# A two-layer hybrid transformer on one core: the first stage's loads, row products and prefills in another order

## The chip, the cores and the metric

The kernel runs on one core of a Trainium2 chip. The metric is the device time of one execution in microseconds (us). Names: PE is TensorE (the matmuls), DVE is VectorE, ACT is ScalarE, SP the engine whose queue issues the loads. On each engine instructions stand in an order that is fixed when the kernel is built.

## The reference, cut to what matters

Two layers work on 512 tokens (256 context, 256 latent) of width 2048. Only the start of the first layer concerns us: from a condition vector come a scale, a shift and a gate per channel, the tokens are normalised, scaled and shifted to `h`, and `h` is multiplied by a wide weight matrix.

```python
def adaln(cond, w, b):
    m = jax.nn.silu(cond) @ w + b
    return jnp.split(m, 3, axis=-1)
...
        shift, scale, gate = adaln(c, w_ada[l], b_ada[l])
        shift_c, scale_c, gate_c = adaln(c_ctx, w_ada[l], b_ada[l])
        h_lat = rms_norm(x, norm_gain[l]) * (1.0 + scale[:, None]) + shift[:, None]
        h_ctx = rms_norm(ctx, norm_gain[l]) * (1.0 + scale_c) + shift_c
...
    a_q, a_ff, a_fb, a_i, b_q, b_k, b_v, b_zf, b_zb, gate = jnp.split(h @ w_in, cuts, axis=-1)
```

All is float32. To keep that precision, an operand of a matmul is split into a high word (a cast) and a low word (what the cast left), and each product is three matmuls: high by high, high by low, low by high.

## The kernel before, in words

The channels form 16 tiles of 128, `h` is held with channels on the partitions, and tile k of `h` can be used as soon as its own scale and shift exist. So the first stage (`with tc.tile_pool(name="startup")`) goes through the tiles in nine chunks (`CHUNKS`, L40): two of one tile, seven of two. For each chunk `ch` the loop of L408 does this:

- **rows** (L312, `mx` is its sum): 16 small float32 matmuls of the condition with the scale and shift columns of this chunk. Their weights are eight tiles `ap`, loaded into a ring of eight buffers (`ADA_BUFS`). From chunk 2 on four column tiles are wanted; three go this way, the fourth as **dots** (L295) on DVE: two loaded tiles `ad`, four products of 128x1024 (`aj`, `ad`).
- **v_mms** (L249): the products of the chunk before with the value weights (`wvh`, `wvl`): 12 matmuls a tile.
- **mods** (L323) and **make_h0** (L349): the row sums are copied to `rs` by ACT, turned by PE, summed by DVE, and give `gs` and `mod`; ACT makes `ht` and its high word `h`, DVE the low word.
- **wave_q** (L367): the chunk before times two more weight tiles (`wqh`, `wql`), 6 matmuls a tile.
- **wave_w** (L359): loads and splits the `wv` and `wq` weights of this chunk for the next turn. There is one buffer for each (`WAVE_BUFS`), so the cast of `wqh` waits until wave_q has read the old one.
- **fill**: work of a later stage, the gate projections, of which `FILL` (L46) lists the part and up to which tile of `h` it goes. It is `proj` (L206) with a weight load (`rawfill`), its cast (`whfill`, ACT) and its low word (`wlfill`, DVE), and three matmuls for each tile, in the order high by high, high by low, low by high.

Before the loop stand the loads of the 16 tiles `x`, the rows of chunk 0, the squares of `x` on ACT (L388), and their sum over the channels on PE (`ss`). All loads go through SP's one queue; the code's order and the builder's scheduler set the order in which they stand, as for every engine.

Of the kernel before, what the change touches and what calls it, by code (L numbers as in the profile page):

```python
# [8 lines left out]
F32 = mybir.dt.float32  # L9
# [8 lines left out]
P = 128  # L18
# [20 lines left out]

CHUNKS = ((0,), (1,), (2, 3), (4, 5), (6, 7), (8, 9), (10, 11), (12, 13), (14, 15))  # L40
WAVE_BUFS = 1
CUT = (0, 4, 0, 0, 0, 0, 0, 0, 0)
SQ_TAGS = ("wh", "wl", "raw", "wh", "wl", "raw", "wh", "wl")
ADA_BUFS = 8
DOT_BUFS = 3
FILL = ((), tuple((p, 2) for p in range(6)), (), ((0, 6), (1, 6)), ((2, 6),), ((3, 8),), ((4, 8),), ((5, 8),), ())  # L46
GLA_WAITS = (4, 2, 2, 3)
NORM_WAITS = {"k": 2, "q": 3}
ATT_WAITS = (6, 2, 3, 2, 2, 2)
# [16 lines left out]
def dit_two_layers(ctx: ExitStack, tc, xT, cc, crow, vecs, w_as, w_as3, w_ad, w_ab, w_wv, w_wq, w_e, w_zz, w_a2, w_eo, w_o, w_oo,  # L66
# [58 lines left out]
        nc.sync.dma_start(raw[:, :n], src)  # L125
        return raw[:, :n]

    def load_split(src, name, eng=None):
        raw = load(src, "raw" + name)
        n = raw.shape[-1]  # L130
        wh = wp.tile([P, 1024], F32R, tag="wh", name="wh" + name, bufs=WH_BUFS)[:, :n]
        wl = wp.tile([P, 1024], F32R, tag="wl", name="wl" + name, bufs=WL_BUFS)[:, :n]
        split(raw, wh, wl, eng)
        return wh, wl
# [63 lines left out]
    def make_h(layer, k, c, t, rstd):  # L198
        seg, shift = segs[c], mod[:, layer, k, c:c + 1]
        dve.scalar_tensor_tensor(t, xt[k][:, seg], gs[:, layer, k, c:c + 1], rstd[:, seg], ALU.mult, ALU.mult)  # L200
        act.activation(hh[k][:, seg], t, AF.Identity, bias=shift)
        dve.scalar_tensor_tensor(hl[k][:, seg], t, shift, hh[k][:, seg].bitcast(F32), ALU.add, ALU.subtract)

    partial = {}

    def proj(units, c0, width, name, h_hi=None, h_lo=None, part=None, k1=KT, eng=None, early=None):  # L206
        a, b = h_hi or hh, h_lo or hl
        sofar, k0 = partial.get(part, (None, 0))
        ps = (acc if k1 == KT else aux)(name)
        for half in range(2):  # L210
            ks, ke = max(k0, 8 * half), min(k1, 8 * half + 8)
            if ks >= ke:
                if k1 == KT:
                    tick(2)
                continue
            o = 8 * half
            wh, wl = load_split(units[half][:, (ks - o) * P:(ke - o) * P], f"{name}_{half}", eng)
            for k in range(ks, ke):
                w1, w2 = wh[:, (k - ks) * P:(k - ks + 1) * P], wl[:, (k - ks) * P:(k - ks + 1) * P]
                x1, x2 = a[k][:, c0:c0 + width], b[k][:, c0:c0 + width]  # L220
                pe.matmul(ps[:, :width], w1, x1, start=(k == k0), stop=False)  # L221
# [56 lines left out]
    with tc.tile_pool(name="startup", bufs=1) as sp:  # L278
# [7 lines left out]
        sb0 = sp.tile([P, 2, D], F32, name="sb0")  # L286
        for c in range(2):
            for j in range(4):
                ps = acc(f"sb0_{c}_{j}")
                for i in range(4):  # L290
                    pe.matmul(ps[:, i * P:(i + 1) * P], view(c32, (4 * j + i) * 32 + c, (0, P)), ident,
                              start=True, stop=True)
                dve.tensor_copy(sb0[:, c, j * T:(j + 1) * T], ps)

        def dots(ch):  # L295
# [16 lines left out]
        def rows(ch, mx, u0, u1):  # L312
            n = len(on_pe(ch)) * P
            for u in range(u0, u1):
                raw = sp.tile([P, 768], F32, tag="ap", name=f"ap{ch}_{u}", bufs=ADA_BUFS)[:, :2 * n]
                nc.sync.dma_start(raw, (w_as if ch < 2 else w_as3)[8 * (ch if ch < 2 else ch - 2) + u])
                for i in range(2):
                    k = u * 2 + i
                    g = 32 * (k % 4)
# [4 lines left out]
        def mods(ch, mx, pd):  # L324
            tiles = on_pe(ch)
            n = len(tiles)
            rs = sp.tile([P, T], F32, tag="rs", name=f"rs{ch}")
            act.copy(rs[:, :n * P], mx[:, :n * P])
            for i in range(n):
                pe.transpose(mx[:, i * P:(i + 1) * P], rs[:, i * P:(i + 1) * P], ident)  # L330
            m4 = sp.tile([P, 4, 2], F32, tag="m4", name=f"m4_{ch}")
            dve.tensor_reduce(m4[:, :n, :], view(mx, 0, (128, n), (1, 2), (32, 4)), AX.X, ALU.add)
            for i, (f, k) in enumerate(tiles):
# [15 lines left out]
        def make_h0(ch):  # L349
            for k in CHUNKS[ch]:  # L350
                new_h(0, k)
                t = sp.tile([P, T], F32, tag="scr", name=f"ht0_{k}", bufs=3)
                for c in range(2):
                    act.activation(t[:, segs[c]], xt[k][:, segs[c]], AF.Identity, bias=mod[:, 0, k, c:c + 1],
# [1 line left out]
                act.copy(hh[k], t)  # L356
                dve.tensor_sub(hl[k], t, hh[k].bitcast(F32))

        def wave_w(ch, what, src, n):  # L359
            k0, nk = CHUNKS[ch][0], len(CHUNKS[ch])  # L360
            src = src[k0 // 2][:, (k0 % 2) * n:(k0 % 2 + nk) * n]
            raw = load(src, f"{what}r{ch}")
            wh, wl = [sp.tile([P, 2 * n], F32R, tag=f"{what}{x}", name=f"{what}{x}{ch}", bufs=WAVE_BUFS)[:, :nk * n]
                      for x in "hl"]
            split(raw, wh, wl, dve)
            return wh, wl

        def wave_q(ch, w2h, w2l):
            for i in range(2):
                for kk, k in enumerate(CHUNKS[ch]):  # L370
# [3 lines left out]
                    pe.matmul(wq[i], w1, hl[k], start=False, stop=False)  # L374
                    pe.matmul(wq[i], w2, hh[k], start=False, stop=(k == KT - 1))

        ss0 = aux("ss0")
        for k in range(KT):
            t = rp.tile([P, T], F32, tag=f"r{(k + 8) % KT}", name=f"x0_{k}")
            nc.sync.dma_start(t, xT[k])  # L380
            xt[k] = t
            if k == 7:
                mx = aux("mx0")
                rows(0, mx, 0, 8)
        for k in range(KT):
            if k % 2 == 0:
                sq = wp.tile([P, 2, T], F32, tag=SQ_TAGS[k // 2], name=f"sq0_{k}", bufs=3)
            act.activation(sq[:, k % 2, :], xt[k], AF.Square)  # L388
            if k % 2 and k < KT - 1:
                dve.tensor_tensor(sq[:, 0, :], sq[:, 0, :], sq[:, 1, :], ALU.add)  # L390
                pe.matmul(ss0, ones, sq[:, 0, :], start=(k == 1), stop=False)
        for i in range(2):
            pe.matmul(ss0, ones, sq[:, i, :], start=False, stop=(i == 1))
        wn = wave_w(0, "wv", w_wv, T), wave_w(0, "wq", w_wq, 256)
# [744 lines left out]
```

## Time and profile before

| | us |
|---|---|
| median of 3 runs | 1758.53 (1756.43 to 1761.26) |
| the profiled execution | 1759.63 |
| its span, first to last instruction | 1757.7 |
| PE busy in the span | 1735.1 (99%) |
| DVE busy | 1283.0 (73%) |
| ACT busy | 760.5 (43%) |

The span is what the profile sees of the execution. A busy time adds the durations of an engine's instructions, in which overlaps count once; a PE matmul is recorded with 0.39 us while the next starts 0.23 us after it, so a busy PE is not yet one at its best. Starts are counted from the start of the span.

### The profile page before, as it was taken

How to read it: one execution, taken by the hardware profiler on the slowest of the kernel's cores; microseconds unless marked ns; L12 is line 12 of the kernel's file. 1: busy time of each engine (PE TensorE's matmuls, PEld its weight loads, DVE VectorE, ACT ScalarE, POOL GpSimd, SP SyncE). 2: the span in 40 equal slices, each digit the busy share in tenths (PEclk: the TensorE clock that was granted, in tenths of full speed). 3: DMA queues.
4: the chain of work that ended last, by engine and by line, in shares of the span. 5: the costliest groups of instructions: out<-in, count | busy, mean ns of one | idle time of the engine just before them, and what ended most of it. 6: DMA issues, size and time to landing. Idle time of an engine off the chain costs nothing.

```text
span 1757.7 us, 24265 instructions
## 1 busy us (share of the span) xinstructions
PE 1735.1 (99%) x9461; PEld 1430.1 (81%) x9461; DVE 1283.0 (73%) x2083; ACT 760.5 (43%) x1111; POOL 66.3 (4%) x85
## 2 busy tenths in 40 slices
PE   8999999999999999999999999999999999999999
PEld 5577888888888888888888888888888888888887
DVE  5565777666676996887999967496595695698665
ACT  5344644244443432434232225453453453567532
POOL 0000100000000000000001110000000000000000
PEclk9999999999999999999999999999999999999999
DMA  8996333433344445456777743332332332334564
GB/s 281 373 358 216 118 117 114 157 126 107 99 146 135 150 155 185 151 186 199 242 268 232 261 158 100 108 108 85 107 103 90 100 116 76 117 120 156 192 211 149
DMA packets 87811, 284.50 MB, mean 162 GB/s; under 512 B 9872, under 2 KB 13712, under 8 KB 87696
## 3 DMA queue, kind: packets, MB, share of 16 engines
q1 hardware_dynamic: 85392, 280.85, 47.8%
q10 hardware_dynamic: 2304, 2.10, 0.4%
q8 instruction: 74, 1.21, 0.3%
q14 instruction: 41, 0.34, 0.1%
HBM read 280.81 MB, written 2.10 MB: 161 GB/s over the span
## 4 chain that ended last, share of the span: by engine, by line
PE 84%; DVE 10%; DMA 2%; ACT 2%; issue 1%; SPq 0%; DVEq 0%; ACTq 0%
PE vo L264 3%; PE vo L266 3%; PE vo L265 3%; PE o L252 3%; PE o L222 3%; PE o L223 3%; PE o L221 3%; PE g L252 3%; PE g L223 2%; PE g L221 2%; PE g L222 2%; PE q L252 2%; PE k L223 2%; PE k L222 2%; PE k L221 2%; PE o L253 2%
## 5 line engine op out<-in xcount | busy, mean ns | idle before, releaser
L451 DVE SCALAR_TENSOR_TENSOR arb<-arb,sb 128x1024 f32<-128x1024 f32 x128 | 163.1, 1278 | 1.7
L106 ACT CAST who<-rawo 128x1024 fp32r<-128x1024 f32 x64 | 67.2, 1051 | 153.6 <-PE o L222 87.8
L451 DVE SCALAR_TENSOR_TENSOR ajb<-arb,sb 128x1024 bf16<-128x1024 f32 x96 | 119.8, 1248 | 0.9 <-ACT sb L176 0.9
L107 DVE TENSOR_TENSOR wlo<-rawo,who 128x1024 fp32r<-128x1024 f32 x64 | 84.9, 1326 | 35.9 <-ACT who L106 34.1
L106 ACT CAST whg<-rawg 128x1024 fp32r<-128x1024 f32 (+1 forms) x61 | 62.1, 1019 | 96.0 <-PE g L222 47.0
L264 PE MATMUL vo<-whvo,h 128*128 128x512 f32 x256 | 100.9, 394 | 0.8 <-DVE qn L902 0.8
L266 PE MATMUL vo<-whvo,h 128*128 128x512 f32 x256 | 100.1, 391 | 0.0
L221 PE MATMUL k<-h,whk 128*128 128x512 f32 x256 | 100.0, 391 | 0.0
L265 PE MATMUL vo<-wlvo,h 128*128 128x512 f32 x256 | 99.9, 390 | 0.0
L223 PE MATMUL k<-h,wlk 128*128 128x512 f32 x256 | 99.8, 390 | 0.0
L222 PE MATMUL k<-h,whk 128*128 128x512 f32 x256 | 99.7, 390 | 0.0
L107 DVE TENSOR_TENSOR wlg<-rawg,whg 128x1024 fp32r<-128x1024 f32 (+1 forms) x61 | 73.6, 1208 | 27.8 <-ACT whg L106 27.6
L252 PE MATMUL g<-h,whg 128*128 128x512 f32 x240 | 85.6, 397 | 0.0
L252 PE MATMUL q<-h,whq 128*128 128x512 f32 x240 | 85.4, 397 | 0.0
L221 PE MATMUL g<-h,whg 128*128 128x512 f32 x214 | 84.1, 393 | 0.0
L223 PE MATMUL g<-h,wlg 128*128 128x512 f32 x214 | 83.6, 391 | 0.0
L222 PE MATMUL g<-h,whg 128*128 128x512 f32 x214 | 83.5, 390 | 0.0
L253 PE MATMUL g<-h,wlg 128*128 128x256 f32 x256 | 69.4, 281 | 0.8 <-DVE wlg L107 0.8
L253 PE MATMUL q<-h,wlq 128*128 128x256 f32 x256 | 69.1, 280 | 0.0
L107 DVE TENSOR_TENSOR wlq<-rawq,whq 128x1024 fp32r<-128x1024 f32 x32 | 39.0, 1222 | 37.8 <-ACT whq L106 37.8
L107 DVE TENSOR_TENSOR wlk<-rawk,whk 128x1024 fp32r<-128x1024 f32 x32 | 39.1, 1223 | 35.4 <-ACT whk L106 35.4
L106 ACT CAST whq<-rawq 128x1024 fp32r<-128x1024 f32 x32 | 33.6, 1051 | 60.2 <-PE k L222 59.9
(553 smaller groups left out, 4954.4 us busy)
## 6 DMA issues: line engine op xcount, KB each, us to landing
arb<-in_w_ab SPq DMA_DIRECT2D x128, 512.0 KB, 4.1
ap<-in_w_as SPq DMA_DIRECT2D x56, 384.0 KB, 7.2
rawo<-in_w_eo SPq DMA_DIRECT2D x32, 512.0 KB, 4.2
rawvo<-in_w_o SPq DMA_DIRECT2D x32, 512.0 KB, 3.5
rawk<-in_w_o SPq DMA_DIRECT2D x32, 512.0 KB, 3.4
rawq<-in_w_o SPq DMA_DIRECT2D x32, 512.0 KB, 3.5
rawg<-in_w_o SPq DMA_DIRECT2D x32, 512.0 KB, 4.1
rawo<-in_w_oo SPq DMA_DIRECT2D x32, 512.0 KB, 4.3
```

Source lines behind the costliest of these rows:

```text
L106: act.copy(dst_hi, src)
L107: r = (eng or dve).tensor_sub(dst_lo, src, dst_hi.bitcast(F32))
L221: pe.matmul(ps[:, :width], w1, x1, start=(k == k0), stop=False)
L222: pe.matmul(ps[:, :width], w1, x2, start=False, stop=False)
L223: pe.matmul(ps[:, :width], w2, x1, start=False, stop=(k == k1 - 1))
L252: pe.matmul(both, w1, hb2[k], start=(k == 0), stop=False)
L253: pe.matmul(ps[:, :NL], w2, hb2[k][:, 0, :], start=False, stop=False)
L264: pe.matmul(pss[t], x1, w1, start=(k == 0), stop=False)
L265: pe.matmul(pss[t], x1, w2, start=False, stop=False)
L266: r = pe.matmul(pss[t], x2, w1, start=False, stop=(k == KT - 1))
L451: dve.scalar_tensor_tensor(dst, raw, 1.0, sb[:, c, :], ALU.mult, ALU.mult, accum_out=o)
```

## The change

It touches only the first stage. Loads are issued by `fetch`, each ordered behind the one before it, and `loads` puts a chunk's `ap` and `ad` loads a whole turn ahead of their use; the loads of the first six prefills get buffers of their own (`early`). The squares of `x` stand ahead of the row copy of chunk 0. Four squares are added on DVE before PE sums them. The rows of a chunk are done in two halves, one ahead of v_mms and one behind it. The first two tiles of `h` are made by `make_h` (scale and shift fused with the normalisation). `FILL` changes: chunk 2 fills two tiles of part 0, chunk 3 now only part 1, chunk 8 four tiles of part 0, 44 tiles in all for 42.

```diff
-CUT = (0, 4, 0, 0, 0, 0, 0, 0, 0)
+SQ_ENDS = (3, 7, 11, 13, 14, 15)
...
-FILL = ((), tuple((p, 2) for p in range(6)), (), ((0, 6), (1, 6)), ((2, 6),), ((3, 8),), ((4, 8),), ((5, 8),), ())
+FILL = ((), tuple((p, 2) for p in range(6)), ((0, 4),), ((1, 6),), ((2, 6),), ((3, 8),), ((4, 8),), ((5, 8),), ((0, 8),))
...
+        def fetch(dst, src):
+
+            with tc.issue_after(queue[0]) if queue[0] is not None else nullcontext():
+                queue[0] = nc.sync.dma_start(dst, src).ins
+
+        def loads(ch, u0, u1):
+            if ch > last:
+                return
+            n = len(on_pe(ch)) * P
+            ad, ap = ada.setdefault(ch, ([], []))
+            for h in range(2 if u0 and len(CHUNKS[ch]) > 1 else 0):
+                ad.append(sp.tile([P, 1024], F32, tag="ar", name=f"ad{ch}_{h}", bufs=DOT_BUFS))
+                fetch(ad[h], w_ad[ch - 2, h])
+            for u in range(u0, u1):
+                ap.append(sp.tile([P, 768], F32, tag="ap", name=f"ap{ch}_{u}", bufs=ADA_BUFS)[:, :2 * n])
+                fetch(ap[u], (w_as if ch < 2 else w_as3)[8 * (ch if ch < 2 else ch - 2) + u])
...
-            act.copy(rs[:, :n * P], mx[:, :n * P])
-            for i in range(n):
-                pe.transpose(mx[:, i * P:(i + 1) * P], rs[:, i * P:(i + 1) * P], ident)
+            with tc.issue_after(squares[13]) if ch == 0 else nullcontext():
+                act.copy(rs[:, :n * P], mx[:, :n * P])
+            with tc.issue_after(sums[3]) if ch == 0 else nullcontext():
+                for i in range(n):
+                    pe.transpose(mx[:, i * P:(i + 1) * P], rs[:, i * P:(i + 1) * P], ident)
...
                 mx = aux(f"mx{ch}")
-                n, cut = 8, CUT[ch]
-                pd = dots(ch)
-                after = rows(ch, mx, 0, n - cut)
-                if cut and ch > 1:
-                    rows(ch, mx, n - cut, n)
-                wn = wave_w(ch, "wv", w_wv, T), wave_w(ch, "wq", w_wq, 256)
-                with tc.issue_after(after):
+                with tc.issue_after(pace[0]) if ch == 2 else nullcontext():
+                    pd = dots(ch)
+                with tc.issue_after(sums[-1]) if ch == 1 else nullcontext():
+                    r = rows(ch, mx, 0, 4)
+                loads(ch + 1, 0, 4)
+                raws = wave_load(ch)
+                with tc.issue_after(r):
                     r = v_mms(wv, *wvw, CHUNKS[ch - 1])
-                if ch == 1:
-                    with tc.issue_after(r):
-                        rows(ch, mx, n - cut, n)
+                with tc.issue_after(r):
+                    r = rows(ch, mx, 4, 8)
+                loads(ch + 1, 4, 8)
+                wn = wave_split(ch, raws)
             mods(ch, mx, pd)
             make_h0(ch)
...
-            for p, k1 in FILL[ch]:
-                proj(w_e[U_GATE + 2 * p:U_GATE + 2 * p + 2], 0, T, f"fill{p}_{k1}", part=p, k1=k1, early=sp)
+            for i, (p, k1) in enumerate(FILL[ch]):
+                with tc.issue_after(first_h) if ch == 1 else nullcontext():
+                    proj(w_e[U_GATE + 2 * p:U_GATE + 2 * p + 2], 0, T, f"fill{p}_{k1}", part=p, k1=k1, early=sp,
+                         raw=early[i] if ch == 1 else None)
```

What this makes of three engines is shown for the turn of chunk 5 (tiles 8 and 9, part 3 of the gate); chunks 3 to 7 read alike. In the names `ad6_1` is the second dots tile of chunk 6, `h0_8` tile 8 of `h`, `wlfill3_8_0` the low word of the fill of part 3.

DVE before, from the turn's `mod` to the next fill's low word (part 4 for chunk 6; that of part 3 stands just ahead of these rows):

```order
L336 TENSOR_SCALAR mod_84<-m4_5_938,vec_75 128x2
L107 TENSOR_TENSOR wvl5_900<-wvr5_897,wvh5_899 128x1024
L305 SCALAR_TENSOR_TENSOR aj6_0_1001,pd6_998<-ad6_0_999,sb0_97 128x1024
L357 TENSOR_TENSOR h0_8_944<-ht0_8_945,h0_8_944 128x512
L107 TENSOR_TENSOR wql5_906<-wqr5_903,wqh5_905 128x512
L305 SCALAR_TENSOR_TENSOR ad6_0_999,pd6_998<-ad6_0_999,sb0_97 128x1024
L357 TENSOR_TENSOR h0_9_950<-ht0_9_951,h0_9_950 128x512
L305 SCALAR_TENSOR_TENSOR aj6_1_1006,pd6_998<-ad6_1_1004,sb0_97 128x1024
L235 TENSOR_TENSOR part3_8_995<-fill3_8_970,part3_2_427 128x512
L305 SCALAR_TENSOR_TENSOR ad6_1_1004,pd6_998<-ad6_1_1004,sb0_97 128x1024
L342 SCALAR_TENSOR_TENSOR mod_84<-pd6_998,vec_75 128x2
L107 TENSOR_TENSOR wlfill4_8_0_1118<-rawfill4_8_0_1115,whfill4_8_0_1117 128x768
```

DVE after the change, the same turn:

```order
L107 TENSOR_TENSOR wvl5_940<-rawwv5_891,wvh5_939 128x1024
L356 TENSOR_SCALAR mod_84<-m4_5_952,vec_75 128x2
L107 TENSOR_TENSOR wql5_944<-rawwq5_893,wqh5_943 128x512
L324 SCALAR_TENSOR_TENSOR aj6_0_1013,pd6_1012<-ad6_0_927,sb0_97 128x1024
L381 TENSOR_TENSOR h0_8_958<-ht0_8_959,h0_8_958 128x512
L324 SCALAR_TENSOR_TENSOR ad6_0_927,pd6_1012<-ad6_0_927,sb0_97 128x1024
L381 TENSOR_TENSOR h0_9_964<-ht0_9_965,h0_9_964 128x512
L324 SCALAR_TENSOR_TENSOR aj6_1_1016,pd6_1012<-ad6_1_929,sb0_97 128x1024
L324 SCALAR_TENSOR_TENSOR ad6_1_929,pd6_1012<-ad6_1_929,sb0_97 128x1024
L362 SCALAR_TENSOR_TENSOR mod_84<-pd6_1012,vec_75 128x2
L107 TENSOR_TENSOR wlfill3_8_0_988<-rawfill3_8_0_985,whfill3_8_0_987 128x768
L235 TENSOR_TENSOR part3_8_1009<-fill3_8_984,part3_2_451 128x512
```

The low word of the turn's own fill stood ahead of the row sum of its turn; now it stands behind that turn's `wql` and behind all four dots of the next chunk.

ACT before, in the same turn:

```order
L106 CAST wvh5_899<-wvr5_897 128x1024
L354 ACTIVATE ht0_8_945<-x0_8_196,mod_84,gs_85 128x256 x2
L354 ACTIVATE ht0_9_951<-x0_9_198,mod_84,gs_85 128x256
L356 CAST h0_8_944<-ht0_8_945 128x512
L106 CAST wqh5_905<-wqr5_903 128x512
L354 ACTIVATE ht0_9_951<-x0_9_198,mod_84,gs_85 128x256
L356 CAST h0_9_950<-ht0_9_951 128x512
L328 COPY rs6_1077<-mx6_997 128x384
L106 CAST whfill4_8_0_1117<-rawfill4_8_0_1115 128x768
```

ACT after the change:

```order
L106 CAST wvh5_939<-rawwv5_891 128x1024
L106 CAST wqh5_943<-rawwq5_893 128x512
L378 ACTIVATE ht0_8_959<-x0_8_179,mod_84,gs_85 128x256 x2
L378 ACTIVATE ht0_9_965<-x0_9_181,mod_84,gs_85 128x256
L380 CAST h0_8_958<-ht0_8_959 128x512
L378 ACTIVATE ht0_9_965<-x0_9_181,mod_84,gs_85 128x256
L380 CAST h0_9_964<-ht0_9_965 128x512
L106 CAST whfill3_8_0_987<-rawfill3_8_0_985 128x768
L347 COPY rs6_1091<-mx6_1011 128x384
```

The cast of `wqh` moved ahead of all `ht`, and the turn's `whfill` from behind the row copy `rs` of its turn to behind the turn's last `h`.

SP before, the loads from the fill of chunk 4 to the `ap` tiles of chunk 5:

```order
L125 DMA rawfill2_6_0_833<-in_w_e 128x512
L302 DMA ad5_0_855<-in_w_ad 128x1024
L302 DMA ad5_1_860<-in_w_ad 128x1024
L316 DMA ap5_0_865<-in_w_as3 128x768
L316 DMA ap5_1_869<-in_w_as3 128x768
L316 DMA ap5_2_873<-in_w_as3 128x768
L316 DMA ap5_3_877<-in_w_as3 128x768
L316 DMA ap5_4_881<-in_w_as3 128x768
L316 DMA ap5_5_885<-in_w_as3 128x768
L316 DMA ap5_6_889<-in_w_as3 128x768
L316 DMA ap5_7_893<-in_w_as3 128x768
L125 DMA wvr5_897<-in_w_wv 128x1024
```

SP after the change, the loads of the turn of chunk 5:

```order
L302 DMA ap6_3_889<-in_w_as3 128x768
L302 DMA rawwv5_891<-in_w_wv 128x1024
L302 DMA rawwq5_893<-in_w_wq 128x512
L302 DMA ad6_0_927<-in_w_ad 128x1024
L302 DMA ad6_1_929<-in_w_ad 128x1024
L302 DMA ap6_4_931<-in_w_as3 128x768
L302 DMA ap6_5_933<-in_w_as3 128x768
L302 DMA ap6_6_935<-in_w_as3 128x768
L302 DMA ap6_7_937<-in_w_as3 128x768
L125 DMA rawfill3_8_0_985<-in_w_e 128x768
L302 DMA ap7_0_1027<-in_w_as3 128x768
```

The fill's load stood ahead of the next chunk's `ad` and `ap`; now it stands behind all of them. Each `ap6` tile takes the buffer of its `ap5` tile, so its load waits in the queue until that row matmul is done.

## Rows read from the trace of the kernel before

**Rows 1.** Stretches: busy time of each engine, granted clock, DMA share, GB/s.

```profile
core 0: us, PE busy (x) PEld busy (x) DVE busy (x) ACT busy (x) POOL busy (x), PEclk, DMA share, GB/s
10.00:20.00 10.00, 10.00 (x74) 5.89 (x74) 4.62 (x8) 3.19 (x7) 0.00 (x0) 1.00 1.05 391
...
94.14:109.79 15.65, 15.65 (x91) 11.29 (x90) 11.56 (x23) 6.01 (x10) 0.00 (x0) 1.00 0.99 363
```

**Rows 2.** PE in order of time: start, duration, instruction, idle before and its releaser.

```profile
29.71 0.80 PE L264 MATMUL wv<-wvh,h 128*128 128x512 f32 x1 [2.43 <-ACT h L356]
...
49.14 2.94 PE L320 MATMUL mx<-ap,c 128*32 128x384 f32 x32
...
56.84 0.84 PE L320 MATMUL mx<-ap,c 128*32 128x384 f32 x4
...
64.49 0.50 PE L264 MATMUL wv<-wvh,h 128*128 128x512 f32 x1
...
94.14 2.79 PE L320 MATMUL mx<-ap,c 128*32 128x384 f32 x32
...
109.79 2.79 PE L320 MATMUL mx<-ap,c 128*32 128x384 f32 x32
...
165.58 0.50 PE L221 MATMUL qA<-h,whqA 128*128 128x512 f32 x1 [0.68 <-ACT vtva L656]
```

**Rows 3.** PE, turn of chunk 5: transposes, wave_q's last, the fill's first and last.

```profile
102.47 0.49 PE L330 MATMUL mx<-cst,rs 128*128 128x128 f32 x3
...
105.37 0.40 PE L375 MATMUL wq<-h,wql 128*128 128x512 f32 x1
105.60 0.39 PE L221 MATMUL fill<-h,whfill 128*128 128x512 f32 x1
...
109.47 0.39 PE L223 MATMUL fill<-h,wlfill 128*128 128x512 f32 x1
```

**Rows 4.** ACT in order of time: the start, and the turn of chunk 5.

```profile
18.64 0.37 ACT L328 COPY rs<-mx 128x256 f32<-128x256 f32 x1 [6.70 <-PE mx L320]
18.91 4.44 ACT L388 ACTIVATE sq<-x 128x512 f32<-128x512 f32 x8
...
97.40 0.84 ACT L106 CAST whfill<-rawfill 128x768 fp32r<-128x768 f32 x1
102.67 1.05 ACT L106 CAST wvh<-wvr 128x1024 fp32r<-128x1024 f32 x1 [4.44 <-PE wv L266]
103.86 1.59 ACT L354 ACTIVATE ht<-x,mod,gs 128x256 f32<-128x256 f32 x3
...
105.87 0.61 ACT L106 CAST wqh<-wqr 128x512 fp32r<-128x512 f32 x1
```

**Rows 5.** DVE in order of time, around the turn of chunk 5.

```profile
97.84 0.22 DVE L342 SCALAR_TENSOR_TENSOR mod<-pd,vec 128x2 f32<-128x2 f32 x1
98.27 0.96 DVE L107 TENSOR_TENSOR wlfill<-rawfill,whfill 128x768 fp32r<-128x768 f32 x1 [0.21 <-ACT whfill L106]
...
106.65 0.68 DVE L107 TENSOR_TENSOR wql<-wqr,wqh 128x512 fp32r<-128x512 f32 x1
107.25 1.22 DVE L305 SCALAR_TENSOR_TENSOR ad<-ad,sb 128x1024 f32<-128x1024 f32 x1
...
108.39 0.69 DVE L357 TENSOR_TENSOR h<-ht,h 128x512 fp32r<-128x512 f32 x1
```

**Rows 6.** An idle time of PE; stretches at the lower clock.

```profile
154.76 0.50 PE L264 MATMUL wv<-wvh,h 128*128 128x512 f32 x1 [2.05 <-ACT h L356]
...
29.42:32.83 3.41, 3.12 (x7) 2.48 (x8) 3.41 (x7) 0.23 (x1) 0.00 (x0) 0.50 1.00 356
...
155.72:159.13 3.41, 3.41 (x10) 2.67 (x9) 2.95 (x3) 1.90 (x3) 0.00 (x0) 0.50 0.43 137
```

**Rows 7.** DMA issues, 80 to 140 us: KB each, median us to landing.

```profile
ap<-in_w_as SPq DMA_DIRECT2D x32, 384.0 KB, 7.4
...
rawfill<-in_w_e SPq DMA_DIRECT2D x3, 384.0 KB, 3.5
```

More of the change, by code (lines that the diff above doesn't have):

```diff
@@ L41 @@
 WAVE_BUFS = 1
-CUT = (0, 4, 0, 0, 0, 0, 0, 0, 0)
-SQ_TAGS = ("wh", "wl", "raw", "wh", "wl", "raw", "wh", "wl")
+SQ_TAGS = ("wh", "wl", "ar", "wh", "wl", "ar", "wh", "wl")
+SQ_ENDS = (3, 7, 11, 13, 14, 15)
 ADA_BUFS = 8
 DOT_BUFS = 3
-FILL = ((), tuple((p, 2) for p in range(6)), (), ((0, 6), (1, 6)), ((2, 6),), ((3, 8),), ((4, 8),), ((5, 8),), ())
+FILL = ((), tuple((p, 2) for p in range(6)), ((0, 4),), ((1, 6),), ((2, 6),), ((3, 8),), ((4, 8),), ((5, 8),), ((0, 8),))
 GLA_WAITS = (4, 2, 2, 3)
@@ L126, in load, with load_split @@
         return raw[:, :n]
-    def load_split(src, name, eng=None):
-        raw = load(src, "raw" + name)
+    def load_split(src, name, eng=None, raw=None):
+        raw = load(src, "raw" + name) if raw is None else raw
         n = raw.shape[-1]
@@ L200, in make_h, with proj @@
         dve.scalar_tensor_tensor(t, xt[k][:, seg], gs[:, layer, k, c:c + 1], rstd[:, seg], ALU.mult, ALU.mult)
-        act.activation(hh[k][:, seg], t, AF.Identity, bias=shift)
+        made[0] = act.activation(hh[k][:, seg], t, AF.Identity, bias=shift).ins
         dve.scalar_tensor_tensor(hl[k][:, seg], t, shift, hh[k][:, seg].bitcast(F32), ALU.add, ALU.subtract)
-    partial = {}
-    def proj(units, c0, width, name, h_hi=None, h_lo=None, part=None, k1=KT, eng=None, early=None):
+    made, partial = [None], {}
+    def proj(units, c0, width, name, h_hi=None, h_lo=None, part=None, k1=KT, eng=None, early=None, raw=None):
         a, b = h_hi or hh, h_lo or hl
@@ L216, in proj @@
             o = 8 * half
-            wh, wl = load_split(units[half][:, (ks - o) * P:(ke - o) * P], f"{name}_{half}", eng)
+            wh, wl = load_split(units[half][:, (ks - o) * P:(ke - o) * P], f"{name}_{half}", eng, raw)
             for k in range(ks, ke):
@@ L288, in dit_two_layers @@
             for j in range(4):
-                ps = acc(f"sb0_{c}_{j}")
+                ps = (aux if (4 * c + j) % 4 == 3 else acc)(f"sb0_{c}_{j}")
                 for i in range(4):
@@ L293, in dit_two_layers @@
                 dve.tensor_copy(sb0[:, c, j * T:(j + 1) * T], ps)
+        ada = {}
+        queue = [None]
+        def fetch(dst, src):
[12 more added lines that the diff above has]
+                fetch(ap[u], (w_as if ch < 2 else w_as3)[8 * (ch if ch < 2 else ch - 2) + u])
         def dots(ch):
@@ L299, in dots @@
             pd = sp.tile([P, 2, 2], F32, tag="pd", name=f"pd{ch}", bufs=2)
-            for h in range(2):
-                raw = sp.tile([P, 1024], F32, tag="ar", name=f"ad{ch}_{h}", bufs=DOT_BUFS)
-                nc.sync.dma_start(raw, w_ad[ch - 2, h])
+            for h, raw in enumerate(ada[ch][0]):
                 junk = sp.tile([P, 1024], BF16, tag="scr", name=f"aj{ch}_{h}", bufs=3)
@@ L314, in rows @@
             for u in range(u0, u1):
-                raw = sp.tile([P, 768], F32, tag="ap", name=f"ap{ch}_{u}", bufs=ADA_BUFS)[:, :2 * n]
-                nc.sync.dma_start(raw, (w_as if ch < 2 else w_as3)[8 * (ch if ch < 2 else ch - 2) + u])
+                raw = ada[ch][1][u]
                 for i in range(2):
@@ L351, in make_h0 @@
                 new_h(0, k)
+                if ch < 2:
+                    for c in range(2):
+                        make_h(0, k, c, sp.tile([P, T], F32, tag="scr", name=f"ht0_{k}_{c}", bufs=3)[:, :NL], rstd)
+                    continue
                 t = sp.tile([P, T], F32, tag="scr", name=f"ht0_{k}", bufs=3)
@@ L357, in make_h0, with wave_load, wave_split @@
                 dve.tensor_sub(hl[k], t, hh[k].bitcast(F32))
-        def wave_w(ch, what, src, n):
+        def wave_load(ch):
             k0, nk = CHUNKS[ch][0], len(CHUNKS[ch])
[L361 to L366, printed above, removed]
+            raws = []
+            for what, src, n in (("wv", w_wv, T), ("wq", w_wq, 256)):
+                raws.append(wp.tile([P, 1024], F32, tag="raw", name=f"raw{what}{ch}", bufs=RAW_BUFS)[:, :nk * n])
+                fetch(raws[-1], src[k0 // 2][:, (k0 % 2) * n:(k0 % 2 + nk) * n])
+            return raws
+        def wave_split(ch, raws):
+            out = []
+            for what, n, raw in zip(("wv", "wq"), (T, 256), raws):
+                wh, wl = [sp.tile([P, 2 * n], F32R, tag=f"{what}{x}", name=f"{what}{x}{ch}",
+                                  bufs=WAVE_BUFS)[:, :raw.shape[-1]] for x in "hl"]
+                split(raw, wh, wl, dve)
+                out.append((wh, wl))
+            return out
         def wave_q(ch, w2h, w2l):
@@ L375, in wave_q @@
                     pe.matmul(wq[i], w2, hh[k], start=False, stop=(k == KT - 1))
+        last = len(CHUNKS) - 1
         ss0 = aux("ss0")
@@ L379, in dit_two_layers @@
             t = rp.tile([P, T], F32, tag=f"r{(k + 8) % KT}", name=f"x0_{k}")
-            nc.sync.dma_start(t, xT[k])
+            fetch(t, xT[k])
             xt[k] = t
+            if k == 7:
+                loads(0, 0, 8)
+        raws = wave_load(0)
+        loads(1, 0, 4)
+        loads(1, 4, 8)
+        early = [sp.tile([P, 1024], F32, tag="ar", name=f"early{i}", bufs=DOT_BUFS) for i in range(2)]
+        early = [early[i // 4][:, i % 4 * 256:(i % 4 + 1) * 256] for i in range(len(FILL[1]))]
+        for (p, _), raw in zip(FILL[1], early):
+            fetch(raw, w_e[U_GATE + 2 * p][:, :256])
+        squares, sums, group = [], [], []
+        for k in range(KT):
+            if k % 2 == 0:
+                sq = (sp if k // 2 in (2, 5) else wp).tile([P, 2, T], F32, tag=SQ_TAGS[k // 2], name=f"sq0_{k}", bufs=3)
+            group.append(sq[:, k % 2, :])
+            with tc.issue_after(squares[-1]) if k else nullcontext():
+                squares.append(act.activation(group[-1], xt[k], AF.Square).ins)
+            if len(group) > 1:
+                dve.tensor_tensor(group[0], group[0], group[-1], ALU.add)
+            if k in SQ_ENDS:
+                sums.append(pe.matmul(ss0, ones, group[0], start=(k == 3), stop=(k == KT - 1)).ins)
+                group = []
             if k == 7:
@@ L384, in dit_two_layers @@
                 rows(0, mx, 0, 8)
[L385 to L394, printed above, removed]
         nc.sync.dma_start(msk, masks)
@@ L397, in dit_two_layers @@
         fn(LNEXP, rstd, rstd, AF.Exp, scale=-0.5)
-        normed(0)
-        normed(1)
+        with tc.issue_after(table["last"]):
+            wn = wave_split(0, raws)
         wv = [acc(f"wv{t}") for t in range(4)]
         wq = [aux(f"wq{t}") for t in range(2)]
-        last = len(CHUNKS) - 1
         pd = None
@@ L407, in dit_two_layers @@
                 mx = aux(f"mx{ch}")
-                n, cut = 8, CUT[ch]
-                pd = dots(ch)
-                after = rows(ch, mx, 0, n - cut)
-                if cut and ch > 1:
-                    rows(ch, mx, n - cut, n)
-                wn = wave_w(ch, "wv", w_wv, T), wave_w(ch, "wq", w_wq, 256)
-                with tc.issue_after(after):
+                with tc.issue_after(pace[0]) if ch == 2 else nullcontext():
[5 more added lines that the diff above has]
+                with tc.issue_after(r):
                     r = v_mms(wv, *wvw, CHUNKS[ch - 1])
-                if ch == 1:
-                    with tc.issue_after(r):
-                        rows(ch, mx, n - cut, n)
+                with tc.issue_after(r):
+                    r = rows(ch, mx, 4, 8)
+                loads(ch + 1, 4, 8)
+                wn = wave_split(ch, raws)
             mods(ch, mx, pd)
             make_h0(ch)
+            if ch == 0:
+                first_h = made[0]
             if 0 < ch < last:
@@ L423, in dit_two_layers @@
             if ch:
-                with tc.issue_after(after):
+                with tc.issue_after(r):
                     wave_q(ch - 1, *wqw)
-            for p, k1 in FILL[ch]:
-                proj(w_e[U_GATE + 2 * p:U_GATE + 2 * p + 2], 0, T, f"fill{p}_{k1}", part=p, k1=k1, early=sp)
+            for i, (p, k1) in enumerate(FILL[ch]):
+                with tc.issue_after(first_h) if ch == 1 else nullcontext():
+                    proj(w_e[U_GATE + 2 * p:U_GATE + 2 * p + 2], 0, T, f"fill{p}_{k1}", part=p, k1=k1, early=sp,
+                         raw=early[i] if ch == 1 else None)
         wvw, wqw = wn
```

## The prediction

> **What bounds the kernel now.** I read the table of busy times first, then the stretches, then PE, ACT and DVE in order of time, and last the DMA issues. PE is busy 99% of the span, so a microsecond in which PE stands idle is a microsecond of the kernel. In the turn of chunk 5, from the rows of chunk 5 to those of chunk 6, PE is busy for all of 15.65 us, DVE for 11.56, ACT for 6.01, and DMA's share is 0.99 [rows 1]. The rows start at 94.14 and 109.79 [rows 2]. So each steady turn is full on PE, and DVE and ACT have some slack, but only as long as what PE wants next is ready when it comes to it. Matmuls of 128x512 follow each other at 0.23 us: the fill's 18 run from 105.60 to 109.47, 17 steps in 3.87 us [rows 3].
>
> The fill needs three things: its load, a cast on ACT, and a low word on DVE. Before, the cast stands at 97.40 [rows 4] and the low word is finished at 98.27 + 0.96 = 99.23 [rows 5]; PE comes to the fill at 105.60 [rows 3]. They are early by over 6 us. This distance is what the change spends.
>
> **The change part by part.** I call E the end of the second half of a chunk's rows, counted on PE.
>
> *The low word.* The order of DVE after the change puts, in the turn of chunk 5, `wlfill` behind `wql` and all four dots of the next chunk. Behind E, PE does the transposes and wave_q, 105.60 - 102.47 = 3.1 us [rows 3]. `wqh` has one buffer, so its cast waits for nearly all of wave_q: it ends at about 2.9 + 0.6 + hand-offs = E + 3.8, its low word `wql` 0.6 later, at E + 4.4 (the next instruction follows `wql` at 107.25 - 106.65) [rows 4, 5]. Then DVE has four dots at 108.39 - 107.25 = 1.14 each, 4.6 in all; two low words of `h` at 0.6, 1.2; one short wait for `h`'s cast, 0.3; the read-outs and `mod`, 0.5: 6.6 us, so E + 11.0 [rows 5]. `wlfill` takes 0.96: it is there at E + 12.0, for the 128x512 ones of parts 1 and 2, which I take at the 0.69 of `h`'s low word of the same size [rows 5], at E + 11.75. PE wants it at E + 3.1.
>
> *The load and the cast.* In SP's order the fill's load now stands behind `ap6_4` to `ap6_7`, and those wait for buffers that the second row half frees, one by one, until E. An issue of such 384 KB lands after 3.5 us for the fill and 7.4 for `ap` [rows 7]; I take E + 7.4, then 0.84 for the cast [rows 4]: E + 8.3. So PE stands from E + 3.1 to E + 8.3, does the two matmuls of the first tile that want only the high word, and stands again to E + 12.0. About 8 us idle a turn.
>
> *What is behind the wait.* In PE's order the next chunk's rows stand behind the fill, so nothing fills these holes. The Trainium skill, "TensorE: Matmul & The Clock Gate", section "Step-by-step: what each phase is for", says that matmuls stay in program order and only weight loads are pulled ahead; no row here shows an overtaking, so the trace neither confirms nor denies it. Where PE did go on past the waiting fill is rival H.
>
> *A turn.* For chunks 5 to 7: half the rows 1.4, 24 matmuls of v 5.6, half the rows 1.4 (rows 2.79 in one piece [rows 2]), 8.4 to E; 12.0; the other 16 matmuls 16 x 0.2325 = 3.7: 24.1 us. For chunks 3 and 4 (four tiles of fill, ten matmuls left, 2.3): 8.4 + 11.75 + 2.3 = 22.4. Chunk 2: 1.4 + 2.8 (one tile of v) + 1.4 = 5.6 to E. Its DVE chain is worked through from the start, since its dots stand behind the turn's other work: row copy and transposes 0.8 [rows 3, 4], row sum, scale and shift with hand-offs 1.0, three `ht` 1.6, `h`'s cast 0.6, `wvh` 1.05 [rows 4], `wvl` 1.2, `wql` 0.6, a low `h` 0.6, dots 4.6, `mod` 0.2, `wlfill` 0.7 [rows 5]: 13.0, with two more hand-offs 13.2. Then four matmuls 0.9: 19.7.
>
> *The clock.* Every wait may cost more than its idle time. After idle times of 2.43 and 2.05 us on PE [rows 2, 6] the granted clock went to 0.50, which is 1.2 GHz, for 3.41 us, and then back to 1.00 [rows 6]; there are three such stretches in all before. In such a stretch matmuls run at half speed, so a full one costs about 3.41 / 2 = 1.7 us, and I take 1.6. For the turns of chunks 2 to 7 I charge one each. The two holes of a turn are 2 to 3 us apart, so the first drop mostly falls on idle time; two drops and none are the bounds.
>
> *The start.* The row copy of chunk 0 stands ahead of the last eight squares on ACT and waits 6.70 us; the squares then take 4.44 [rows 4]. Now the squares stand ahead. Between 0 and 6.70 us can be had; DMA's share is 1.05 from 10 to 20 us [rows 1], so the squares wait for `x` in part instead, and PE does three `ss` matmuls fewer. I take 3.6, a bit over half. Rows of chunk 2 start at 49.14 - 3.6 = 45.5 [rows 2].
>
> *The end of the stage.* Chunk 8 from its rows to the first `qA`: rows 1.4, v 5.6, rows 1.4, transposes and wave_q 3.1, a gap I put at 1.3 while the row copy stands behind a cast of `whqA` on ACT (one of 1.05 [rows 4] and hand-offs), fill 12 x 0.23 = 2.8, v of chunk 8 5.6, its wave_q 2.8, its copy out, put at 0.8: 24.8. Before: rows of chunk 8 at 94.14 + 3 x 15.65 = 141.1, `qA` at 165.58 [rows 2], 24.5. Two more tiles are filled early, so the later stage has six matmuls less, 1.4.
>
> *The sum.* Rows of chunk 3 at 45.5 + 19.7 + 1.6 = 66.8; of chunk 5 at 66.8 + 2 x (22.4 + 1.6) = 114.8 (94.14 before); of chunk 8 at 114.8 + 3 x (24.1 + 1.6) = 191.9 (141.1 before); `qA` at 216.7, 51.1 later than 165.58. With -1.4: +49.7. The profiled execution took 1759.63, 1.1 above the median, so 1809.3 for it; the 1.1 are less than the terms are sure to, and I give 1809.
>
> DVE's own price is from rows. The Trainium skill, "VectorE: DVE Perf Modes", sections "Specifications" and "Mode 1× (REGULAR) — the baseline", gives 0.96 GHz and one result a cycle, 1.07 us for 1024 elements as an estimate. That would make four dots 0.3 us shorter a turn and the kernel 2 us faster over six turns; the trace has 1.14 from start to start, and the trace decides.
>
> **The rivals.**
>
> *A, faster.* `wlfill` is ready by E + 3.1 after all: DVE does its dots elsewhere, as it does before the change, and the load is early. Then turns are PE's again, 15.65 for chunks 5 to 7. The gains remain: 3.6 at the start; the rows of chunk 3, which now run from 56.84 to 64.49 instead of 2.8 us [rows 2], lose 4.9 to late loads, of which 2.9 (again a bit over half) may come back; 1.4, since chunks 2 and 3 fill six tiles instead of eight; less 0.3 at the end of the stage; and the 1.4 of the later stage: -9.0, 1750.6. It decides where the low word comes before E + 3.1. The order on DVE speaks against it: the dots of the next chunk stand ahead, and they stand behind a cast that waits for wave_q.
>
> *B, only the load binds.* Dots cost the fill nothing, the low word follows the cast: E + 8.3 + 0.9 = E + 9.2 instead of 12.0, six times 2.8 less, 1792.
>
> *C and D, the clock.* Two drops a turn give 6 x 1.6 = 9.6 more, 1819; none gives 1800. For C speaks that each turn has two holes longer than those before which the clock fell; for D that a drop can fall on the second hole.
>
> *F, the clock stays down* for whole turns: 54 matmuls at half speed take 54 x 0.23 = 12.4 more a turn, 6 x (12.4 - 1.6) = 65 more, 1874. The three stretches, all of one length and with busy PE behind them, speak against it.
>
> *H, PE goes on past the waiting fill* with the next chunk's first row half and v, 1.4 + 5.6 = 7.0 us of the 8 idle: 6 x 7.0 = 42 less, 1767. The two waits at v in the rows of before [rows 2, 6] show PE simply idle.
>
> *G, nothing changes*: what the turns lose is made up where DMA has been ahead. With PE at 99% there is nothing to make up 50 us from.
>
> **How the numbers follow.** Forecast 61%, C 14%, D 12%, B 4%, F 3%, A 3%, G 2%, H 1%. The time is the forecast's, 1809. The range runs from 1791 (B at 1792, or D with all of the 6.70 at the start, 1797) to 1823 (C with none of it, 1822.6): it leaves out A, F, G and H, and a part of the uncertain sums. Faster by over 0.3% is A, 0.03; G is 0.02; slower is all else, 0.95. 0.3% is about what a measurement of this kernel can tell from no change: its three runs span 4.8 us.
>
> **What would show it.** In the profile after: in each turn of chunks 2 to 7 two idle times of PE ahead of the fill, the first of about 5 us (from chunk 3 on), released by `whfill` on ACT, the second of about 3.2, released by `wlfill` on DVE; busy time of PE nearly as before, its share down to about 96%; DVE's four dots in one row ahead of `wlfill`; rows of chunk 8 at about 192 and `qA` at about 217; DMA's share in these turns well below the 0.99. Stretches at 0.50 once a turn decide between forecast, C, D and F. I would be wrong if PE did other work while the fill waits, or if the low word came to it by another way than the order on DVE shows.

## The result and the profile after

The changed kernel takes 1815.73 us (1815.27 to 1817.38) and the kernel before 1759.03 beside it: 1.0325 times as long, interval 1.0307 to 1.0342, 56.7 us slower. The forecast was 1809, within 1791 to 1823.

The page's busy times after the change (share of the span, instructions), then its waits of PE from 0 to 230 us (the line that waited, for whom, us in total, times, longest):

```profile
PE 1745.7 (96%) x9455; PEld 1434.6 (79%) x9455; DVE 1287.8 (71%) x2091; ACT 760.5 (42%) x1109; POOL 66.6 (4%) x85
```

```profile
PE fill L221 <- ACT whfill L106: 44.3, 6, 10.7
PE sb L291 <- ACT c L168: 4.2, 1, 4.2
PE fill L221 <- ACT h L201: 4.2, 1, 4.2
PE fill L223 <- DVE wlfill L107: 3.5, 5, 0.9
```

The fill waits six times for its cast, 44.3 us together, and then five times for its low word, 3.5. Before, the fill of the steady turns did not wait at all [rows 3]. The span has grown by 57.9 us, from 1757.7 to 1815.6: 47.3 of them are idle time of PE, and 10.6 are busy time, which is the lower clock, below.

The turn of chunk 5 after the change, PE in order of time (answers to [rows 2, 3]):

```profile
127.91 1.50 PE L338 MATMUL mx<-ap,c 128*32 128x384 f32 x16
130.13 0.49 PE L350 MATMUL mx<-cst,rs 128*128 128x128 f32 x3
140.16 0.79 PE L221 MATMUL fill<-h,whfill 128*128 128x512 f32 x1 [7.43 <-ACT whfill L106]
140.75 0.63 PE L222 MATMUL fill<-h,whfill 128*128 128x512 f32 x1
141.88 0.79 PE L223 MATMUL fill<-h,wlfill 128*128 128x512 f32 x1 [0.50 <-DVE wlfill L107]
...
148.21 1.50 PE L338 MATMUL mx<-ap,c 128*32 128x384 f32 x16
```

The same turn on ACT, on DVE (answers to [rows 4, 5]) and in the load queue, SP:

```profile
131.25 1.05 ACT L106 CAST wvh<-rawwv 128x1024 fp32r<-128x1024 f32 x1 [1.27 <-DMA rawwv<-in_w_wv]
132.53 0.62 ACT L106 CAST wqh<-rawwq 128x512 fp32r<-128x512 f32 x1 [0.23 <-PE wq L406]
...
139.28 0.83 ACT L106 CAST whfill<-rawfill 128x768 fp32r<-128x768 f32 x1 [2.31 <-DMA rawfill<-in_w_e]
```

```profile
133.60 0.69 DVE L107 TENSOR_TENSOR wql<-rawwq,wqh 128x512 fp32r<-128x512 f32 x1
134.20 1.22 DVE L324 SCALAR_TENSOR_TENSOR aj<-ad,sb 128x1024 bf16<-128x1024 f32 x1
...
139.47 1.23 DVE L324 SCALAR_TENSOR_TENSOR ad<-ad,sb 128x1024 f32<-128x1024 f32 x1
...
140.88 0.95 DVE L107 TENSOR_TENSOR wlfill<-rawfill,whfill 128x768 fp32r<-128x768 f32 x1
```

```profile
128.78 2.57 SPq L302 DMA_DIRECT2D ap<-in_w_as  x4
131.45 0.39 SPq L125 DMA_DIRECT2D rawfill<-in_w_e  x1
```

E is 127.91 + 1.43 = 129.34 here (the next matmul follows 1.43 us after such a half in this trace: 103.37 to 104.80 in the turn ahead). The cast ends at E + 10.8, the low word is used at E + 12.5. ACT's releaser is the load, and between `wql` and `wlfill` DVE is never idle for more than 0.42 us: both things that the prediction named are there, and they end within 2 us of each other (the cast at 140.11, the low word at 141.83). The stretches of this turn (columns of [rows 1]):

```profile
120.77:148.21 27.44, 19.51 (x90) 12.90 (x89) 10.36 (x19) 6.19 (x10) 0.00 (x0) 0.81 0.53 196
133.50:139.00 5.50, 0.00 (x0) 0.00 (x0) 5.08 (x10) 3.21 (x6) 0.00 (x0) 0.81 0.70 274
140.16:148.21 8.05, 7.55 (x18) 5.21 (x18) 1.63 (x4) 0.00 (x0) 0.00 (x0) 0.56 0.00 0
```

27.44 us instead of 15.65, DMA at 0.53 instead of 0.99. From 133.50 to 139.00 PE does nothing and DVE is busy for 5.08 of 5.50 us, mostly with the dots. While the fill runs at last, DMA moves nothing at all (0.00): the next loads wait for buffers that only the rows behind the fill free. These rows start at 148.21, and the next load is issued at 149.09.

### The profile page after: what moved, and what is told of

Same layout as the page of the kernel before. It is cut to its first block, busy times and chain, and to the rows that moved or that the text cites. A ratio compares the mean times of both kernels' runs of the same rounds, so it can differ in the third digit from the quotient of the medians.

```text
span 1815.6 us, 24282 instructions
## 1 busy us (share of the span) xinstructions
PE 1745.7 (96%) x9455; PEld 1434.6 (79%) x9455; DVE 1287.8 (71%) x2091; ACT 760.5 (42%) x1109; POOL 66.6 (4%) x85
## 4 chain that ended last, share of the span: by engine, by line
PE 83%; DVE 10%; DMA 3%; ACT 2%; issue 2%; SPq 1%; DVEq 0%; ACTq 0%
PE vo L266 3%; PE vo L265 3%; PE vo L264 3%; PE o L252 3%; PE o L222 3%; PE o L223 3%; PE o L221 3%; PE g L252 3%; PE g L223 2%; PE g L221 2%; PE g L222 2%; PE q L252 2%; PE k L223 2%; PE k L222 2%; PE k L221 2%; PE o L253 2%
## 5 line engine op out<-in xcount | busy, mean ns | idle before, releaser
L221 PE MATMUL fill<-h,whfill 128*128 128x512 f32 x44 | 24.6, 562 | 48.5 <-ACT whfill L106 44.3
```

## The experiments

**Two causes, each alone and both.** The prediction had a late load and dots in the way. In the changed kernel they cannot be told apart, since cast and low word come nearly together. The first run takes away the dots, the second the late load.

```diff
-                with tc.issue_after(pace[0]) if ch == 2 else nullcontext():
+                with tc.issue_after(pace[0]) if ch >= 2 else nullcontext():
                     pd = dots(ch)
```

> The changed kernel with one edit: from chunk 3 on the four dots stand behind the fill's low word on DVE (before: only chunk 2's were held). The load stays late. Theory (two things in parallel hold the fill, the late load and the dots; the later one counts): in the changed kernel the low word came 0.5 to 0.9 us after PE had used up the high word, so only about 1.2 us of a turn can go, over five turns about 6 us: 1809 to 1811. Rival 1 (the dots alone are the cause, as the sum of the prediction used them): the low word would come about 5 us earlier a turn, 1785 to 1792. Rival 2 (the two row halves or the clock cost the time, not the fill's words): 1815 to 1816, no change.

Measured: 1809.19 us (1804.54 to 1810.95), ratio 1.0279 (1.0261 to 1.0298); 6.5 less than the changed kernel. PE's waits in it:

```profile
PE fill L221 <- ACT whfill L106: 42.3, 6, 10.2
```

The waits for the low word are gone, those for the cast stay. With the load late, the dots are worth only what they come later than the load.

```diff
+                if ch > 1:
+                    pre = []
+                    for p, k1 in FILL[ch]:
+                        k0 = partial[p][1]
+                        pre.append(wp.tile([P, 1024], F32, tag="raw", name=f"rawfill{p}_{k1}", bufs=RAW_BUFS)[:, :(k1 - k0) * P])
+                        fetch(pre[-1], w_e[U_GATE + 2 * p][:, k0 * P:k1 * P])
                 loads(ch + 1, 0, 4)
```

> The changed kernel with one edit: the fill's load of chunk ch is fetched in the program's queue order ahead of the first four row weights of chunk ch+1, instead of behind all eight. Nothing else is written differently; the order on DVE and ACT then puts the fill's cast and low word ahead of h and of the dots by itself. Theory: both holes of PE in chunks 3 to 7 close, turns go back to about 14.3 (chunks 3 and 4) and 15.7 us (5 to 7); from 226.0 for the first qA to about 160 to 168, 1750 to 1760. Rival 2 (row halves, clock): turns stay above 20 us, over 1790. Rival 3 (the load is early but DMA is then behind for the rows, as it was before in chunk 3): PE waits at the rows instead, 1765 to 1785.

Measured: 1758.27 us, ratio 0.9993 (0.9983 to 1.0002): all that was lost is back. The turn of chunk 5 on DVE in it:

```profile
104.00 0.22 DVE L356 TENSOR_SCALAR mod<-m,vec 128x2 f32<-128x2 f32 x1
104.13 0.95 DVE L107 TENSOR_TENSOR wlfill<-rawfill,whfill 128x768 fp32r<-128x768 f32 x1
...
111.88 1.22 DVE L324 SCALAR_TENSOR_TENSOR aj<-ad,sb 128x1024 bf16<-128x1024 f32 x1
```

But this run moved two things: with the load early, the builder itself put the low word ahead of the dots. So it does not say what an early load alone gives. The next run keeps the early load and orders the low word behind the dots.

```diff
+            if 2 <= ch < last:
+                pd_next = dots(ch + 1)
+                hold[0] = lastdot[0]
             for i, (p, k1) in enumerate(FILL[ch]):
...
+        with tc.issue_after(hold[0]) if hold[0] is not None else nullcontext():
+            r = (eng or dve).tensor_sub(dst_lo, src, dst_hi.bitcast(F32))
```

> As the run with the early load alone, but the fill's low word is ordered behind the four dots of the next chunk, as in the changed kernel (the dots themselves are the same). The load and the cast are early, only the dots are in the way. Theory (each of the two alone is enough to hold the fill): wvl, wql, then four dots of 1.14 us, then the low word, about 12 to 14 us behind the second row half: one long wait of PE at the low word in each turn of chunks 3 to 7, 1810 to 1824. Rival 1 of the opposite kind (the load alone is the cause, dots are harmless once it is early): 1750 to 1762.

Measured: 1768.62 us, ratio 1.0049 (1.0032 to 1.0065). My expectation of 1810 to 1824 was wrong by over 40 us, and the rival's 1762 is also passed. The low word is as late as expected; PE's order is what I had not thought of. PE in the turn of chunk 4 in this run:

```profile
98.45 0.39 PE L223 MATMUL fill<-h,whfill 128*128 128x512 f32 x1
98.68 0.40 PE L224 MATMUL fill<-h,whfill 128*128 128x512 f32 x1
99.01 1.50 PE L342 MATMUL mx<-ap,c 128*32 128x384 f32 x16
101.79 1.21 PE L266 MATMUL wv<-wvh,h 128*128 128x512 f32 x4 [1.28 <-ACT wvh L107]
...
109.24 0.50 PE L225 MATMUL fill<-h,wlfill 128*128 128x512 f32 x1
```

```profile
108.09 0.69 DVE L109 TENSOR_TENSOR wlfill<-rawfill,whfill 128x512 fp32r<-128x512 f32 x1
```

The builder had moved the rest of the fill behind the next chunk's row half and v. The low word, done at 108.09 + 0.69 = 108.78 on DVE, is wanted at 109.24, and the only wait left in this turn is 1.28 us for `wvh`. The next run forbids this move.

```diff
-                with tc.issue_after(sums[-1]) if ch == 1 else nullcontext():
+                with tc.issue_after(sums[-1] if ch == 1 else end[0]):
                     r = rows(ch, mx, 0, 4)
```

Here `end[0]` is the last matmul of the fill.

> As the run with the early load and the dots ahead of the low word, with one more order: on PE the next chunk's rows stand behind the fill, as in the changed kernel (the run before let them move ahead of it). DVE's order from the row sum to the low word is now that of the changed kernel, row for row; only the load is early. Theory (order on PE and dots on DVE together make the wait; the late load is not needed for it): the low word comes about 11.7 us behind the second row half, turns of 22 to 25 us, 1806 to 1814. Rival (the late load is needed): 1755 to 1770.

Measured: 1816.88 us, ratio 1.0331 (1.0314 to 1.0349), 2.9 above the range that I gave: the whole loss, without the late load. PE's waits, then PE and the low word on DVE in the same turn:

```profile
PE fill L225 <- DVE wlfill L109: 47.5, 6, 8.4
```

```profile
108.74 0.39 PE L223 MATMUL fill<-h,whfill 128*128 128x512 f32 x1
108.97 0.40 PE L224 MATMUL fill<-h,whfill 128*128 128x512 f32 x1
117.12 0.79 PE L225 MATMUL fill<-h,wlfill 128*128 128x512 f32 x1 [7.76 <-DVE wlfill L109]
```

```profile
116.38 0.69 DVE L109 TENSOR_TENSOR wlfill<-rawfill,whfill 128x512 fp32r<-128x512 f32 x1
```

The high word is there at once, the low word 7.76 us later. So, with the fill ahead of the next rows on PE: late load alone 1809, dots alone 1817, both 1816, neither 1758. (In the run with neither, the builder kept this order in chunks 4 to 7, and mixed the fill with the next rows in chunks 2 and 3.) The two causes lie side by side, and either makes nearly the whole loss. Between the last two runs only PE's order differs on purpose (1768.62 and 1816.88), and it carries 48 us; the builder's order on DVE moved a little with it, the low words of `h` from ahead of the dots to between them.

**The fill a turn later.** The changed kernel, with the matmuls of the fills of chunks 2 to 7 placed behind the second row half of the next chunk, the load where it was:

```diff
             for i, (p, k1) in enumerate(FILL[ch]):
+                if 1 < ch < last:
+                    k0 = partial[p][1]
+                    due.append((p, k1, load_split(w_e[U_GATE + 2 * p][:, k0 * P:k1 * P], f"fill{p}_{k1}_0")))
+                    continue
...
                 with tc.issue_after(r):
                     r = rows(ch, mx, 4, 8)
+                while due:
+                    p, k1, words = due.pop()
+                    with tc.issue_after(r):
+                        proj(None, 0, T, f"fill{p}_{k1}", part=p, k1=k1, early=sp, words=words)
```

> The changed kernel with the fill's matmuls of chunks 2 to 7 placed on PE behind the second row half of the next chunk; its load and cast stay in their place in the code, so the load stays behind all eight row weights of the next chunk. Theory (what costs is that the rows and v stand behind the waiting fill on PE, not that its words are late): the words are then early enough, turns 16 to 19 us, 1760 to 1785. Rival (PE waits for the words wherever the fill stands, because the load queue itself has fallen behind): still over 1800.

Measured: 1758.64 us, ratio 0.9998 (0.9988 to 1.0007), 1.4 us below the range that I gave. No wait for a fill's word is left in chunks 2 to 7. The load queue as such had not fallen behind. This run does not part the two causes either, since the use moved away from both.

**What the change can be worth.** Four runs build on the early load. The first also puts the value and query weights ahead of the next chunk's row weights, and the dots behind the low word:

```diff
-                loads(ch + 1, 0, 4)
                 raws = wave_load(ch)
+                loads(ch + 1, 0, 4)
```

> Early load, dots behind the low word, and in each turn the loads of the value and query weights ahead of the next chunk's first four row weights (they stood behind). In the changed kernel PE waits 4.20 us in chunk 1 for h, whose scale stands on DVE behind the low words of value weights that land at 37.3 us. Theory: these land some 4 us earlier, the wait shrinks by 2 to 4 us, and the rest is as with the early load: 2 to 4 us below that run. Rival: the rows of chunk 2 then wait for their own loads instead, and the time is that of the early load alone.

Measured: 1756.53 us, ratio 0.9983 (0.9974 to 0.9992), 1.7 below the run with the early load, a little less than expected. The wait in chunk 1 falls from 4.2 us (2.6 with the early load) to 1.0, and chunk 2 waits 3.5 for its own `h`, for 2.4 with the early load alone. So part of the gain went into the next wait. The next two change this version in one place each: the list of fills for chunks 2 and 3, and the rows in one piece.

```diff
-FILL = (..., ((0, 4),), ((1, 6),), ((2, 6),), ...)
+FILL = (..., (), ((0, 6), (1, 6)), ((2, 6),), ...)
```

> The version with the early loads of fill, value and query weights, and the list of fills for chunks 2 and 3 as it was before the change: nothing in chunk 2, two parts of four tiles in chunk 3; chunk 8 as changed. In that version PE waits 3.5 us in chunk 2 for h of the same chunk before its fill. Theory: this wait goes, 2 to 3 us less than 1756.5: 1753 to 1755. Rival (DMA is what chunks 2 and 3 wait for; PE then waits at the rows instead): 1756 to 1758.

Measured: 1752.17 us, ratio 0.9961 (0.9946 to 0.9976), a bit better than expected.

```diff
-                    r = rows(ch, mx, 0, 4)
+                    r = rows(ch, mx, 0, 8)
...
-                with tc.issue_after(r):
-                    r = rows(ch, mx, 4, 8)
```

> The version with the early loads of fill, value and query weights, but all eight row weights of a chunk are used in one piece ahead of v, as before the change. In that version a steady turn takes 16.0 us, before the change 15.65, and the rows 1.50 twice instead of 2.79 once. Theory: turns go back to about 15.7, six times 0.3, 2 us less: 1754 to 1755. Rival (one piece needs all eight weights half a turn earlier, so PE waits for DMA as it did in chunk 3 before the change): 1757 to 1762.

Measured: 1750.84 us, ratio 0.9957 (0.9943 to 0.9972), 3 us better than expected: the turns are back at 15.64 (rows at 89.16 and 104.80), and the rows of chunk 2 start at 44.08 for 45.85 in the version with two halves. Both edits together:

> Both of the edits that helped, together: early loads of fill, value and query weights, dots behind the low word, the rows in one piece, and the list of fills for chunks 2 and 3 as before the change. The first qA came at 160.8 with the list and at 159.4 with the one piece, at 165.1 without either. Theory: each took away a wait of its own (2 to 3.5 us at the fill of chunk 2, 0.3 us of rows in every turn), so they add up in part: 1747 to 1750. Rival (chunks 2 and 3 are bound by DMA, which both only uncover): 1750 to 1752, as with either alone.

Measured: 1751.04 us, ratio 0.9951 (0.9937 to 0.9964): no better than either, as the rival had it. PE in order of time, rows of chunk 3 in the last run:

```profile
57.42 3.79 PE L338 MATMUL mx<-ap,c 128*32 128x384 f32 x16 [2.69 <-DMA ap<-in_w_as]
```

With both waits gone, the rows of chunk 3 wait 2.69 us for their weights, and from 44 to 60 us DMA's share is 1.03. In the versions with one edit it is 1.00 (the list) and 1.03 (the one piece) there, so both edits seem to come up against the same bound; no run tests this by itself. These last three versions beat the kernel before by 7 to 9.5 us.

## Why the prediction was right, and where its sizes were off

**The mechanism was right**, and the runs showed it: fill words that come some 12 us behind E on an engine that cannot go on without them. The prediction saw both causes, and it priced rival B (only the load binds) at 17 us below the forecast. The run without the dots shows 6.5 below the changed kernel: the load was nearly as late as the dots. That the total came so near is in part luck: in chunks 3 to 7 the two idle times of a turn add to 7.1 to 7.9 us, for 8.2 to 8.4 in the forecast, and the lower clock cost more than it was charged.

**By its steps**, first `qA` 216.7 predicted and 226.0 measured:

- *The start*, +4.1. Rows of chunk 2 were to come at 45.5, and came at 49.63, no earlier than before [rows 2]. The squares did go ahead, and PE reached the transposes of chunk 1 at 33.84 for 36.12 before, but these 2.3 us and more went into a wait of 4.20 in chunk 1: `fill <- ACT h`. The value weights for that chunk land at 37.3 us, behind row weights in the queue, and `mod` stands behind their low words on DVE. The run with the early load alone leaves them there: PE gets to the fill later and waits only 2.57, but starts it at 40.63 (40.53 in the changed kernel), and the rows of chunk 2 at 49.62. The run with these loads ahead started the rows of chunk 2 at 45.85, so this is shown. It was the step that failed: I priced the squares and did not follow what was late next.
- *Chunk 2*, 19.7 + 1.6 = 21.3 predicted, 21.40 measured (49.63 to 71.03), in part by luck: the low word ended at E + 13.5 for 13.2, but PE's one wait there, 10.74, is for the cast, whose load was issued at 60.27, 4.8 behind E. The last four matmuls at the lower clock cost 0.9 more than at the full one, for the 1.6 charged. *Chunks 3 and 4*, 24.0 each predicted, 25.2 and 24.5 measured.
- *Chunks 5 to 7*, 25.7 predicted, 27.44, 27.02 and 27.14 measured. In chunk 5 the 1.7 are: 0.2 to E (8.57 for 8.36), 0.5 at the low word (E + 12.5 for 12.0, since `wvh` waited 1.27 for its load, and with it `wvl` and `wql` on DVE), 1.0 at the clock.
- *The load and cast* were to end at E + 8.3 and ended at E + 10.8: the load was issued 2.1 behind E, at 131.45, since the issues of four row weights stood ahead of it from 128.78 to 131.35, and it landed 7.8 us later. I had counted the 7.4 from E. This made one hole of 7.43 and one of 0.50 out of the forecast's 5 and 3.2. Their sum, 7.9, I had as 8.4.
- *The clock* was mis-sized. I charged 1.6 us a turn, and expected PE's busy time nearly as before; it grew by 10.6. After the low word came, 16 matmuls of the fill of chunk 5 took 148.21 - 141.88 = 6.33 us, for 3.72 at full clock: 2.6. The granted clock was 0.56 from 140.16 to 148.21. It is nearer to rival C's price, though not by its two drops: PE's matmuls show one low stretch a turn, with the idle time ahead of it.
- *Chunk 8*, 24.8 predicted, 23.7 measured. Behind the stage the changed kernel won back 2.5 (the spans differ by 57.9, `qA` by 60.4) for 1.4 predicted.

Errors of +4.1, +6.3 in the turns, -1.1 and -1.1 add to 8.2; the profiled execution took 1817.38, 8.1 more than 1809.3.

**The rivals.** A, D, F, G and H did not come about: no turn ran at 15.65, the clock fell in every turn of chunks 2 to 7 (granted 0.78 to 0.86 over a turn), no stretch stayed low for whole turns, and PE stood idle from 132.73 to 140.16 with the next rows ready behind the fill (the first four weights were issued from 121.65 to 123.40 and landed at most 7.3 us later). The Trainium skill, "TensorE: Matmul & The Clock Gate", section "Step-by-step: what each phase is for", says that matmuls stay in program order. Here the trace agrees: no matmul starts between 108.97 and 117.12 in the run with the fill first, and the run that puts the next rows ahead in program order starts them at 99.01, right behind the fill's first two matmuls, and is 48 us faster.

## What to carry to other kernels

Extra work that fills an in-order engine must have its operands ready before the engine gets there, or stand behind the work that must go on; count for it the distance from load to use, through the load queue and through each engine's order. When an edit moves loads, look at what the builder then does on the other engines: here one load placed earlier moved the low word ahead of four dots, and both together were worth 57 us. When two causes end within a microsecond or two of each other, taking away one shows little; test each with the other gone.

## What was not expected of the hardware

After waits of about 7 us, PE came back at the lower granted clock and stayed there for most of the fill: 18 matmuls took 8.05 us with 0.50 idle, for about 4.2 before [rows 3]. In the turn of chunk 5 PE is busy for 19.51 us where it was 15.65 [rows 1], and over the whole span 10.6 us longer, with nearly the same work. A fill's load of 384 KB issued behind four row weights landed 7.8 us later; before, the fill's loads of that size took 3.5 [rows 7].
